# Memory keys and values by one plain float32 product in place of three rounded ones, in a two-layer streaming encoder step

## The chip, the cores and the metric

One NeuronCore of one Trainium2 chip runs the whole step as a single program. The metric is device time in microseconds (us). Its engines are named as the profile names them: PE (matmul; PEld are its weight loads), DVE (vector), ACT (scalar, with its own instruction queue), POOL (GpSimd, which also issues DMAs on a software queue) and SP (which issues only DMAs).

## The reference, cut to what matters

Two layers run over 512 prompt tokens and 32 sample tokens. Both layers attend into 256 memory rows, and the memory's keys and values for both layers come from one function, which does not depend on the tokens:

```python
def memory_kv(mem, mem_norm_g, w_mem_kv, mem_k_norm_g):
    Bsz, M, _ = mem.shape                      # M = 256, D = 1024
    m = rms_norm(mem[None], mem_norm_g[:, None, None, :])
    kv = jnp.einsum('lbmd,ldk->lbmk', m, w_mem_kv)   # 2 layers, 1024 -> 512
    k, v = jnp.split(kv, 2, axis=-1)
    k = rms_norm(k.reshape(DEPTH, Bsz, M, MEM_HEADS, MEM_HEAD_DIM), ...)
    return k, v.reshape(DEPTH, Bsz, M, MEM_HEADS, MEM_HEAD_DIM)
```

Everything is float32. The prompt's memory attention of layer 0 needs layer 0's keys and values, that of layer 1 needs layer 1's; both are outputs too.

## The kernel before, in words

Large products are made in three parts. A float32 operand is rounded to the one-instruction format float32r (the high part) and the rest is kept as a second float32r tile (the low part); the product is high by high, high by low and low by high, added in PSUM. For a weight tile, `weights` (L227) does this: SP loads the raw tile into a slot of the ring `wraw`, ACT writes the high part (L231) and the negated rounded copy (L232), and POOL issues a second DMA of the same weights that adds itself onto that copy (L233). The raw slot is put back at once, the high and low slots (rings `whi`, `wlo`) after the matmuls. Each ring has three slots.

The program's first stretch projects the tokens into layer 0 (`z0`, L324). Then comes the state-space stage (S5) of layer 0: six groups `m`, and for each a chain of small matmuls and transposes on PE (L681, L700, L729, L739, L752, L791, L792, L803), evacuations on ACT, table products and a scan on DVE (L669 to L696, L763 to L780), and a kernel matrix that POOL writes to DRAM (`kd<-kp`, L710) and reads back in eight small DMAs (L719) before the output products L791. After the last group the outputs are split, layer 0 attends into the memory (L430 to L520), and the product with `w_glu` starts the long dense part of the program: output projection, feed-forward, layer 1, feed-forward.

`mem_kv` (L334) is a generator whose pieces fill the S5 stage. Eight units (four pairs of 128 feature rows, two layers) each scale a pair of memory tiles by the norm's gain on ACT into a high part (L344), make the low part on DVE (L345), fetch a weight tile through `weights`, and issue 12 matmuls of 128 by 512 columns (L350): two row blocks, two feature tiles, three parts. That makes 96. Four PSUM banks collect the sums over all eight units. An epilogue then normalises the rows, writes both outputs and transposes the keys (L364 to L409).

The order on each engine is not the source order: a planner in the compiler orders the instructions by priority and by its own costs. The table `ORDER` moves blocks: the units of `mem_kv` have -60 (later than their place), its epilogue `mem_kv_end` 580 (earlier), the scans `s5_scan` 400. Engines then run their queues strictly in that order.

The memory units take their row tiles from the ring `rb`: four float32r tiles of 512 columns, made at L1004.

Of the kernel before, what the change touches and what calls it, by code (L numbers as in the profile page):

```python
# [9 lines left out]
F32 = mybir.dt.float32  # L10
F32R = mybir.dt.float32r
I32 = mybir.dt.int32
AF = mybir.ActivationFunctionType
ALU = mybir.AluOpType
# [4 lines left out]
KD = D // 128  # L19
# [8 lines left out]
NMEM = 256  # L28
# [109 lines left out]
def body(ctx, tc, A, O):  # L138
    nc = tc.nc
    V, S, P, T = nc.vector, nc.scalar, nc.gpsimd, nc.tensor  # L140
# [3 lines left out]
    FW = 576  # L144

    def slots(pool, n, dt, w, name):
        return Slots([pool.tile([128, w], dt, name=f"{name}{i}") for i in range(n)])
# [3 lines left out]
    R = None  # L151
    WR = slots(base, 3, F32, 1024, "wraw")
# [53 lines left out]
    def gcol(name, i):  # L206
        c = GP[name] + i
        return gp[:, c:c + 1]
# [18 lines left out]
    def weights(ap, *n, lo_eng=None):  # L227

        raw, hi, lo = WR.get(*n), WH.get(*n), WL.get(*n)
        nc.sync.dma_start(raw, ap)  # L230
        S.activation(hi, raw, AF.Copy)  # L231
        S.activation(lo, raw, AF.Copy, scale=-1.0)  # L232
        P.dma_start(lo, ap, accum_op=ALU.add)  # L233
        WR.put(raw)
        return hi, lo
# [8 lines left out]
    def wfree(w):  # L244
        WH.put(w[0])
        WL.put(w[1])
# [79 lines left out]
    def combos(a, b):  # L326
        return ((a[0], b[0]), (a[0], b[1]), (a[1], b[0]))
# [6 lines left out]
    def mem_kv(fm, rm, bm, b1, dst):  # L334
        ps = [[bm.get(512) for _ in range(2)] for _ in range(2)]
        acc = fm.get(2, NMEM)
        for u in range(4):
            mt = fm.get(2, NMEM)
            nc.sync.dma_start(mt, A["mem"][:, 2 * u:2 * u + 2, :])
            for l in range(2):  # L340
                hi, lo = rm.get(2, NMEM), rm.get(2, NMEM)
                for k2 in range(2):
                    g = gcol("mem", l * KD + 2 * u + k2)
                    S.activation(hi[:, k2], mt[:, k2], AF.Copy, scale=g)  # L344
                    V.scalar_tensor_tensor(lo[:, k2], mt[:, k2], g, hi[:, k2].bitcast(F32), ALU.mult, ALU.subtract)  # L345
                w = weights(A["w_mkv"][l, u], 1024, lo_eng=V if l else P)
                for t in range(2):
                    for k2 in range(2):
                        for i, (x, ww) in enumerate(combos((hi, lo), w)):
                            T.matmul(ps[l][t], x[:, k2, 128 * t:128 * t + 128], ww[:, 512 * k2:512 * k2 + 512],  # L350
                                     start=u == 0 and k2 == 0 and i == 0, stop=u == 3 and k2 == 1 and i == 2)
                wfree(w)
                rm.put(hi, lo)
                if l:
                    if u:
                        q = fm.get(2, NMEM)
                        S.activation(q, mt, AF.Square)
                        P.tensor_tensor(acc, acc, q, ALU.add)
                        fm.put(q)
                    else:  # L360
                        S.activation(acc, mt, AF.Square)
                    fm.put(mt)
                yield
        b = b1.get(512)  # L364
        for t in range(2):
            for u in range(2):
                T.matmul(b[:, t:t + 1], acc[:, u, 128 * t:128 * t + 128], ones, start=u == 0, stop=u == 1)
        x = sm(2, "mx", 1)
        V.tensor_scalar(x, b[:, :2], 1.0 / D, EPS, ALU.mult, ALU.add)
        b1.put(b)  # L370
        fm.put(acc)
        r = rsqrt(x, 128, 2, "mrs")
        yield
        for l in range(2):
            kt, v = dst[l]
            ss = sm(8, "mss")
            q = fm.get(2, 256)
            for t in range(2):
                S.activation(q[:, t], ps[l][t][:, :256], AF.Square, scale=r[:, t:t + 1])
                S.activation(v[:, t, :], ps[l][t][:, 256:], AF.Copy, scale=r[:, t:t + 1])  # L380
            V.tensor_reduce(ss, view(q, [[64, 8], [1, 64]]), AX.X, ALU.add)
            P.dma_start(O["mem_v"][l].rearrange("t p c -> p t c"), v)
            yield
            x = sm(8, "mkx")
            V.tensor_scalar(x, ss, 1.0 / 64, EPS, ALU.mult, ALU.add)
            y = rsqrt(x, 128, 8, "mkr")
            fm.put(q)
            V.tensor_tensor(y.rearrange("p (t h) -> p t h", t=2), y.rearrange("p (t h) -> p t h", t=2),
                            view(r, [[1, 2], [0, 4]]), ALU.mult)
            yield  # L390
            kk = fm.get(2, 256)
            for t in range(2):
                V.tensor_tensor(kk[:, t].rearrange("p (h d) -> p h d", d=64),
                                ps[l][t][:, :256].rearrange("p (h d) -> p h d", d=64),
                                view(y, [[1, 4], [0, 64]], 4 * t), ALU.mult)
            bm.put(*ps[l])
            kf = view(kk, [[64, 8], [1, 64]])
            V.tensor_tensor(kf, kf, view(grow(f"mk{l}"), [[0, 8], [1, 64]]), ALU.mult)
            P.dma_start(O["mem_k"][l].rearrange("t p c -> p t c"), kk)
            yield  # L400
            pt = b1.get(512)
            for hp in range(2):
                for t in range(2):
                    T.transpose(pt[:, 256 * hp + 128 * t:256 * hp + 128 * t + 128],
                                kk[:, t, 128 * hp:128 * hp + 128], ident)
            S.activation(kt.rearrange("p a b -> p (a b)"), pt, AF.Copy, scale=mqg[:, l:l + 1])
            b1.put(pt)
            fm.put(kk)
            yield  # L409
# [504 lines left out]
    lr = exr.enter_context(tc.tile_pool(name="l0r", bufs=1, reuse_waits="tile"))  # L914
    R = slots(lr, 16, F32R, NT, "ra")
# [73 lines left out]
    with pri("norm0"):  # L989
        rb = norm_bcast(r0, BS)  # L990
# [10 lines left out]
    exr.close()  # L1001
    exr = ExitStack()
    lr = exr.enter_context(tc.tile_pool(name="l0b", bufs=1, reuse_waits="tile"))
    R, fx = slots(lr, 4, F32R, 512, "rb"), slots(lr, 3, F32, FW, "fx")  # L1004
    FA, FB, FD = slots(lr, 2, F32, 1024, "wv"), slots(lr, 1, F32, 2 * FW, "tb"), slots(lr, 3, F32, 2 * FW, "wc")
    fxs = list(fx.free)
    F.merge(fx)
# [64 lines left out]
    lr = ctx.enter_context(tc.tile_pool(name="rc", bufs=1, reuse_waits="tile"))  # L1072
    R = slots(lr, 16, F32R, NT, "rc")
    bh = sm(NM, "bh", 1)
    V.tensor_scalar(bh, gp[:, GP["bglu"]:GP["bglu"] + NM], 0.5, None, ALU.mult)
    for y in ys:
        hi, lo = R.get(NT), R.get(NT)
# [7 lines left out]
    for m in range(NM):  # L1085
        if m in (1, 2, 4, 5):
            unit("mem_attend0", att)
        ps = BS.get(512), BS.get(512)
# [11 lines left out]
    for m in range(NM):  # L1100
        hi, lo = R.get(NT), R.get(NT)
# [38 lines left out]
    r1, rb = None, None  # L1140
    for m in range(8):
        ps = BG.get(512), BG.get(512)
        gemm(ps, xs, weights(A["w_in"][1, m], 1024))
        if rb is None:
            with pri("norm1"):
                r1, rb = norm_rows([acc], BM)
        if m < NM:
            hi, lo = R.get(NT), R.get(NT)
            sqt = zacc if m == 0 else F.get(NT)
            g = gcol("ql", m)  # L1150
# [21 lines left out]
    ps = BM.get(512)  # L1172
    stat_cols(zacc, ps)
    F.put(zacc)
    x = sm(5, "qx", 1)
# [625 lines left out]
```

## Time and profile before

| | us |
|---|---|
| median of three runs | 1451.76 (1451.24 to 1459.61) |
| the profiled execution, its own time | 1449.85 |
| span of that execution in the trace | 1448.1 |
| PE busy in the span | 1403.1 (97%) |
| DVE, ACT, POOL busy | 723.6, 755.9, 388.6 |

The profiled execution is 1.9 us under the median. A busy PE is not PE at its peak: matmuls overlap each other's fill and drain. PE is nearly full over the whole span but not over the stretch in which the memory projection lies, so its total share says little of this change. Stretches are given in us from the start of the span.

### The profile page before, as it was taken

How to read it: one execution, taken by the hardware profiler on the slowest of the kernel's cores; microseconds unless marked ns; L12 is line 12 of the kernel's file. 1: busy time of each engine (PE TensorE's matmuls, PEld its weight loads, DVE VectorE, ACT ScalarE, POOL GpSimd, SP SyncE). 2: the span in 40 equal slices, each digit the busy share in tenths (PEclk: the TensorE clock that was granted, in tenths of full speed). 3: DMA queues.
4: the chain of work that ended last, by engine and by line, in shares of the span. 5: the costliest groups of instructions: out<-in, count | busy, mean ns of one | idle time of the engine just before them, and what ended most of it. 6: DMA issues, size and time to landing. Idle time of an engine off the chain costs nothing.

```text
span 1448.1 us, 26899 instructions
## 1 busy us (share of the span) xinstructions
PE 1403.1 (97%) x10693; PEld 1310.7 (91%) x10693; DVE 723.6 (50%) x1810; ACT 755.9 (52%) x1247; POOL 388.6 (27%) x676
## 2 busy tenths in 40 slices
PE   7978799999999999999989999999999999999998
PEld 6966689999999999999988987557999999999998
DVE  7989742455514551455257655663355513551351
ACT  6656555565535553556555554654555534553452
POOL 2155432322111211124325421432322211221121
PEclk8999889999999999999999999999999999999999
DMA  9754637778788888869742432002778887888875
GB/s 268 163 142 121 155 75 175 169 164 175 176 179 171 176 176 178 173 141 207 158 120 62 124 102 60 11 20 57 165 171 177 177 175 172 176 177 174 176 157 139
DMA packets 67198, 214.80 MB, mean 148 GB/s; under 512 B 9280, under 2 KB 11552, under 8 KB 67072
## 3 DMA queue, kind: packets, MB, share of 16 engines
q0 software_dynamic: 30304, 100.81, 38.5%
q1 hardware_dynamic: 35616, 110.17, 26.5%
q10 hardware_dynamic: 1152, 2.10, 0.4%
q8 instruction: 84, 1.38, 0.4%
q14 instruction: 42, 0.34, 0.1%
HBM read 207.41 MB, written 5.61 MB: 147 GB/s over the span
## 4 chain that ended last, share of the span: by engine, by line
PE 82%; DVE 2%; DMA 2%; ACT 2%; issue 2%; POOL 1%; DVEq 0%; POOLq 0%; ACTq 0%
PE bank L324 64%; PE bank L1308 2%; PE bank L1556 2%; PE bank L1395 2%; PE bank L1592 1%; PE bank L1509 1%; PE bank L1483 1%; PE bank L1581 1%; DMA wlo<-i_w_f 1%; PE bank L1197 1%; PE bank L482 1%; PE bank L520 1%; PE bank L1423 1%; PE bank L510 0%; PE bank L1364 0%
## 5 line engine op out<-in xcount | busy, mean ns | idle before, releaser
L324 PE MATMUL bank<-rc,whi 128*128 128x272 f32 x3728 | 628.9, 290 | 0.2 <-DVE rc L305 0.2
L324 PEld LDWEIGHTS bank<-rc,whi 128*128 128x128 f32 x3728 | 530.3, 189 | 5.3 <-issue 4.3
L324 PE MATMUL bank<-rc,wlo 128*128 128x272 f32 x1864 | 389.4, 289 | 0.0
L231 ACT ACTIVATE whi<-wraw 128x1024 fp32r<-128x1024 f32 (+2 forms) x186 | 191.5, 1029 | 360.1 <-issue 311.3
L324 PEld LDWEIGHTS bank<-rc,wlo 128*128 128x128 f32 x1864 | 294.0, 189 | 0.4 <-issue 0.2
L324 PE MATMUL bank<-g,whi 128*128 128x272 f32 x1408 | 234.6, 288 | 0.8 <-ACT g L216 0.8
L324 PEld LDWEIGHTS bank<-g,whi 128*128 128x128 f32 x1408 | 198.8, 188 | 1.3 <-ACT g L216 1.2
L233 POOL DMA_DIRECT2D wlo<-i_w_f x136 | 117.5, 864 | 303.8 <-ACT wlo L232 300.5
L232 ACT ACTIVATE wlo<-wraw 128x1024 fp32r<-128x1024 f32 (+2 forms) x186 | 189.1, 1017 | 3.9 <-PE bank L350 3.3
L324 PE MATMUL bank<-g,wlo 128*128 128x272 f32 x704 | 145.8, 288 | 1.8 <-DMA wlo<-i_w_f 1.6
L851 DVE SCALAR_TENSOR_TENSOR fa<-fa,gp,fa 128x546 f32<-128x546 f32 x88 | 69.7, 792 | 139.8 <-ACT fa L850 139.8
L865 DVE TENSOR_TENSOR h<-bank,h 128x272 f32<-128x272 f32 x96 | 38.2, 436 | 172.3 <-PE bank L324 171.9
L324 PEld LDWEIGHTS bank<-g,wlo 128*128 128x128 f32 x704 | 110.4, 188 | 2.2 <-DMA wlo<-i_w_f 2.2
L850 ACT ACTIVATE fa<-fa,gp 128x546 f32<-128x546 f32 x88 | 73.2, 832 | 12.8 <-DVE fa L845 12.8
L843 DVE TENSOR_TENSOR fa<-bank,fa 128x272 f32<-128x272 f32 x88 | 38.9, 443 | 81.7 <-PE bank L324 77.5
L852 DVE SCALAR_TENSOR_TENSOR fa<-fa,gp,fa 128x546 f32<-128x546 f32 x88 | 69.5, 790 | 3.1
L891 ACT ACTIVATE fa<-fa 128x546 f32<-128x546 f32 x44 | 29.2, 663 | 71.7 <-DVE fa L852 71.7
L847 POOL COPY fa<-gp 128x2 f32<-128x2 f32 x88 | 19.0, 216 | 168.3 <-DVE g L217 107.7
L848 POOL COPY fa<-fa 128x4 f32<-128x4 f32 x88 | 18.2, 207 | 165.2 <-DVE fa L845 165.2
L324 PE MATMUL bank<-ra,whi 128*128 128x272 f32 x256 | 47.5, 307 | 3.1 <-ACT whi L241 3.1
L216 ACT ACTIVATE g<-fa 128x544 fp32r<-128x544 f32 x44 | 29.0, 659 | 37.6 <-DVE fa L893 37.6
L892 DVE TENSOR_TENSOR fa<-fa,fa 128x512 f32<-128x512 f32 x44 | 30.5, 693 | 33.6 <-ACT fa L891 33.6
(629 smaller groups left out, 2020.3 us busy)
## 6 DMA issues: line engine op xcount, KB each, us to landing
wraw<-i_w_f SPq DMA_DIRECT2D x120, 512.0 KB, 4.9
wlo<-i_w_f POOLq DMA_DIRECT2D x120, 512.0 KB, 7.4
wraw<-i_w_out SPq DMA_DIRECT2D x16, 512.0 KB, 4.3
wlo<-i_w_out POOLq DMA_DIRECT2D x16, 512.0 KB, 7.1
wraw<-i_w_in SPq DMA_DIRECT2D x14, 512.0 KB, 5.0
wlo<-i_w_in POOLq DMA_DIRECT2D x14, 512.0 KB, 7.7
wraw<-i_w_f SPq DMA_DIRECT2D x16, 384.0 KB, 3.4
wlo<-i_w_f POOLq DMA_DIRECT2D x16, 384.0 KB, 6.3
```

What stands on the lines that cost most here:

```text
L216: S.activation(hi, src, AF.Copy)
L231: S.activation(hi, raw, AF.Copy)
L232: S.activation(lo, raw, AF.Copy, scale=-1.0)
L233: P.dma_start(lo, ap, accum_op=ALU.add)
L324: T.matmul(ps[q][:, :c], ww, xx[:, c0:c0 + c], start=k == 0 and i == 0, stop=k == n - 1 and i == 2)
L843: V.tensor_tensor(u[:, 2:274], ps[0][:, :272], rb[:, :272], ALU.mult)
L850: S.activation(y, u[:, 2:548], AF.Identity, scale=gcol("cw", 3 * ci + 2), bias=gcol("cb", ci))
L851: V.scalar_tensor_tensor(y, u[:, 1:547], gcol("cw", 3 * ci + 1), y, ALU.mult, ALU.add)
L852: V.scalar_tensor_tensor(y, u[:, 0:546], gcol("cw", 3 * ci), y, ALU.mult, ALU.add)
L865: V.tensor_tensor(h[m][:, c0:c0 + cc], ps[qd][:, :cc], h[m][:, c0:c0 + cc], ALU.add)
L891: S.activation(yg, yg, AF.Silu)
L892: V.tensor_tensor(u[:, 2:514], ya[:, :NP], yg[:, :NP], ALU.mult)
```

## The change

The row tiles are scaled into one plain float32 tile, the raw weight tile is loaded and used as it is, and each product is one float32 matmul call in place of three float32r ones. The low part of the rows (DVE), the two conversions of the weights (ACT) and the adding DMA (POOL) of this projection go. The raw weight slot is put back after the matmuls of its unit and no longer right after the conversions; the rings of high and low weights aren't used here any more. The ring `rb` becomes two float32 tiles. All other products keep their three parts.

```diff
             for l in range(2):
-                hi, lo = rm.get(2, NMEM), rm.get(2, NMEM)
+                x, w = rm.get(2, NMEM), WR.get(1024)
+                nc.sync.dma_start(w, A["w_mkv"][l, u])
                 for k2 in range(2):
-                    g = gcol("mem", l * KD + 2 * u + k2)
-                    S.activation(hi[:, k2], mt[:, k2], AF.Copy, scale=g)
-                    V.scalar_tensor_tensor(lo[:, k2], mt[:, k2], g, hi[:, k2].bitcast(F32), ALU.mult, ALU.subtract)
-                w = weights(A["w_mkv"][l, u], 1024, lo_eng=V if l else P)
+                    S.activation(x[:, k2], mt[:, k2], AF.Copy, scale=gcol("mem", l * KD + 2 * u + k2))
                 for t in range(2):
                     for k2 in range(2):
-                        for i, (x, ww) in enumerate(combos((hi, lo), w)):
-                            T.matmul(ps[l][t], x[:, k2, 128 * t:128 * t + 128], ww[:, 512 * k2:512 * k2 + 512],
-                                     start=u == 0 and k2 == 0 and i == 0, stop=u == 3 and k2 == 1 and i == 2)
-                wfree(w)
-                rm.put(hi, lo)
+                        T.matmul(ps[l][t], x[:, k2, 128 * t:128 * t + 128], w[:, 512 * k2:512 * k2 + 512],
+                                 start=u == 0 and k2 == 0, stop=u == 3 and k2 == 1)
+                WR.put(w)
+                rm.put(x)
...
-    R, fx = slots(lr, 4, F32R, 512, "rb"), slots(lr, 3, F32, FW, "fx")
+    R, fx = slots(lr, 2, F32, 512, "rb"), slots(lr, 3, F32, FW, "fx")
```

## Rows read from the trace of the kernel before

**Rows 1.** The page: span, busy time of the engines.

```profile
span 1448.1 us, 26899 instructions
PE 1403.1 (97%) x10693; PEld 1310.7 (91%) x10693; DVE 723.6 (50%) x1810; ACT 755.9 (52%) x1247; POOL 388.6 (27%) x676
```

**Rows 2.** Windows: length, busy of PE, PEld, DVE, ACT, POOL, clock, DMA.

```profile
72.00:96.70 24.70, 17.98 (x148) 15.15 (x145) 24.54 (x43) 12.41 (x29) 12.94 (x24) 0.86 0.60 142
102.10:150.20 48.10, 40.63 (x403) 32.92 (x398) 47.86 (x78) 31.68 (x75) 29.37 (x49) 1.00 0.58 136
150.20:168.00 17.80, 13.97 (x101) 11.87 (x101) 12.67 (x42) 9.38 (x25) 9.13 (x17) 0.90 0.69 174
66.00:168.00 102.00, 83.30 (x769) 69.03 (x767) 90.53 (x170) 63.99 (x146) 55.61 (x97) 0.95 0.60 143
184.00:1448.00 1264.00, 1249.83 (x9469) 1178.05 (x9468) 568.12 (x1413) 644.57 (x1026) 316.36 (x547) 1.00 0.66 145
```

**Rows 3.** Groups by shape, 60 to 215 us: removed ACT and POOL work.

```profile
L232 ACT ACTIVATE wlo<-wraw 128x1024 fp32r<-128x1024 f32 x7 | 7.4, 1061 | 2.0 <-PE bank L350 2.0
L231 ACT ACTIVATE whi<-wraw 128x1024 fp32r<-128x1024 f32 x7 | 7.4, 1057 | 3.3 <-issue 2.5 <-PE bank L350 0.6 <-ACT fx L361 0.2
L233 POOL DMA_DIRECT2D wlo<-i_w_mkv x7 | 6.5, 936 | 13.8 <-ACT wlo L232 13.8
```

**Rows 4.** Timeline of DVE: start, duration, instruction, idle before and releaser.

```profile
102.11 0.45 DVE L763 TENSOR_TENSOR fa<-bank,tab 128x276 f32<-128x276 f32 x1 [5.38 <-ACT wlo L232]
...
112.14 0.48 DVE L345 SCALAR_TENSOR_TENSOR rb<-fa,gp,rb 128x256 fp32r<-128x256 f32 x1
112.54 0.69 DVE L672 TENSOR_TENSOR wv<-wv,tb 128x512 f32<-128x512 f32 x1
...
147.48 1.50 DVE L345 SCALAR_TENSOR_TENSOR rb<-fa,gp,rb 128x256 fp32r<-128x256 f32 x1
148.90 1.34 DVE L696 TENSOR_TENSOR wc<-wc,tb 128x1152 f32<-128x1152 f32 x1
```

**Rows 5.** Window of line L345 alone: DVE busy and its count.

```profile
60.00:215.00 155.00, 8.65 (x16) 0.91 0.53 127
```

**Rows 6.** Timeline of PE: three-part products, memory projection; first w_glu matmul.

```profile
98.07 0.87 PE L350 MATMUL bank<-whi,rb 128*128 128x512 f32 x3
98.78 0.40 PE L350 MATMUL bank<-wlo,rb 128*128 128x512 f32 x1
...
184.01 0.82 PE L324 MATMUL bank<-rc,whi 128*128 128x272 f32 x2
```

**Rows 7.** Groups by shape, 870 to 1000 us: plain float32 products.

```profile
L1556 PE MATMUL bank<-fe,fa 96*128 96x512 f32 x4 | 2.0, 592 | 0.0
L1556 PE MATMUL bank<-fe,fa 96*128 96x128 f32 x4 | 0.8, 274 | 0.0
```

**Rows 8.** Line L449: min/median/max ns, first and last start.

```profile
L449 PE MATMUL bank<-fa,fa x8: 379/379/462, 171.3 to 889.3; 128*128 128x256 f32 x8
```

**Rows 9.** Waits from 66 to 168 us: total, times, longest.

```profile
POOL fa L719 <- DMA kd<-kp: 18.6, 4, 6.7
```

**Rows 10.** Timeline of POOL around the fifth kernel matrix.

```profile
137.41 0.61 POOL L710 DMA_DIRECT2D kd<-kp  x1 [0.30 <-POOL kp L707]
...
140.43 3.56 POOL L719 DMA_DIRECT2D fa<-kd  x6 [0.35 <-issue]
```

**Rows 11.** The chain that ended last: start, us, piece.

```profile
140.18 0.94 ACT whi L231
...
144.17 1.82 PE bank L350 x7
...
152.03 4.42 DMA kd<-kp
...
157.00 4.63 DMA fa<-kd
```

**Rows 12.** Timeline of SP's queue: start, us, DMA issues, count.

```profile
144.49 26.49 SPq L230 DMA_DIRECT2D wraw<-i_w_glu  x4
```

## The prediction

> **What bounds the kernel now.** I read the page first. PE is busy for 97% of the span, so one expects that anything which lengthens PE's work lengthens the kernel, and that work on other engines is free [rows 1]. That holds for the dense part, where PE is busy for 1249.83 of 1264 us. The windows show that it does not hold where the changed lines are [rows 2]. All the memory matmuls lie between 72 and 168 us. From 66 to 168 us PE is busy for 83.3 of 102 us and DVE for 90.5; from 72 to 96.7 us DVE is busy for 24.54 of 24.70 us, and from 102.1 to 150.2 us for 47.86 of 48.10. In these two stretches DVE is the bound: the table products and scans of the six groups queue there back to back, and the low parts of the memory rows stand between them. Between the two DVE waits 5.38 us for the first product of the third group [rows 4]. After 150 us DVE has room again, and the last kernel matrix's way through DRAM sets the end [rows 11].
>
> So the change takes work from the stage's bound and gives work to the engine that is next to it. The question is how much of what DVE gives back PE takes.
>
> **PE.** Before, the projection is 96 matmuls of 512 columns. Undisturbed they start 0.237 us apart: three from 98.07 to 98.78 us [rows 6]. That is 96 x 0.237 = 22.8 us. After, there are 32 products in plain float32. The trace has no such product of 128 by 128 by 512, but it has smaller ones. Line L449 issues two products in each of two layers, four in all, and shows eight instructions: a plain product is two instructions [rows 8]. In L1556 the instruction takes 592 ns at 512 columns and 274 at 128, so a column costs (592 - 274) / 384 = 0.828 ns and 512 columns 0.424 us [rows 7]. The part that doesn't grow overlaps with the neighbour, as it does in L350, where matmuls of 0.40 us start every 0.237 us. I take 0.433 us, the slope and 9 ns of spacing; the lower end is 0.424, the upper 0.592 if nothing overlaps. 64 x 0.433 = 27.7 us, which is 4.9 us more than before (4.3 to 15.1). In rows 66 to 168 us PE rises to 88.2 us and DVE falls to 81.9: PE becomes the busiest engine of the stage.
>
> The Trainium skill has a rule by which this term has the other sign: "Perfetto Trace Analysis", section Engine Utilization, gives the matmul rate with a footnote that float32 in its low-and-high form runs at half the rate, as one reads it two cycles for a column of a product. By it the 32 products would be 32 x 0.433 = 13.9 us and PE 8.9 us lighter. The eight instructions for four products speak against reading it for a whole product, and for reading it for each of two [rows 8]; its time is a rival below.
>
> **DVE.** The sixteen instructions of L345 go, 8.65 us of busy time [rows 5]. What they hold of the queue is the step to the next start: 0.40 us (112.14 to 112.54), and once 1.42 us, at 147.48, where it ran slowly [rows 4]. Five of them lie in the first full stretch: 5 x 0.40 = 2.0 us. Eight lie in the second: 7 x 0.40 + 1.42 = 4.2 us. Three lie after 150 us, where DVE is busy for 12.67 of 17.80 us; they are worth nothing [rows 2].
>
> In the first stretch PE is busy for 17.98 of 24.70 us, and a sixth of its added work, 0.8 us, fits: I take the 2.0 us whole. In the second PE stands at 40.63 us. About half of the memory matmuls are there, so it gets some 2.5 us more: 43.1 us. If the stretch shrank by all of 4.2 us to 43.9, PE would have to be 98% busy, as full as in the dense part, in a stretch where it waits for ACT and DVE between small matmuls. If PE reached only 91.5%, midway between today's 84% and the dense part's 99%, the stretch would be 47.1 us and the gain 1.0. I take the middle of 1.0 and 4.2, which is 2.6 us.
>
> **The 5.38 us stall.** The row names a weight conversion on ACT as what ended it [rows 4]. ACT runs in order, and a conversion of 1.06 us ahead of an evacuation holds up the transposes, the scan's products and so DVE. Without conversions ACT is free there, but PE's memory matmuls stand in the same chain and get longer by about a quarter. Bounds: 0 to 5.4 us; I take 0, since the one conversion (1.06) and the added matmul time are of one size.
>
> **ACT and POOL.** Seven conversions of each kind from 60 us on, 14 x 1.06 = 14.8 us of ACT, and seven adding DMAs, 6.5 us of POOL, go [rows 3]. Neither is the bound: 63.99 and 55.61 us of 102 [rows 2]. The bytes go too. POOL's queue waits 18.6 us in four times for the kernel matrix to land in DRAM, at worst 6.7 us [rows 9]. With no adding DMA near, the fifth goes out at 137.41 and its reads begin at 140.43, at most 3.0 us later [rows 10]. So the round trips of the early groups should shorten by 2 to 4 us each. What hides that today is DVE's queue: group outputs wait for the scan. I cost it at 0, and it is worth up to what the stall rival takes.
>
> **The end of the stage.** On the chain from 137.50 to 162.11 us stand 16 memory matmuls in five pieces, the longest 1.82 us [rows 11]. They would cost 16 x 0.237 = 3.8 us before, and 16 / 3 x 0.866 = 4.6 after: 0.8 us more. The conversion at 140.18, 0.94 us, leaves the same chain. Sum -0.1 us. The chain then runs through the last matrix, 4.42 us to DRAM and 4.63 us back, which the change doesn't touch.
>
> **The moved release.** A raw weight slot is now held until its unit's matmuls. SP issues in order, so the loads of `w_glu` queue behind the third last, second last and last unit. Before, four such loads went out between 144.49 and 170.98 us [rows 12], while the first matmul that needs any starts at 184.01 [rows 6]. A load that waits until the last unit, at 166 us, is no later than the last of these. Cost 0; if the projection slipped past 175 us, its delay would come through. Two tiles in place of four in the ring `rb` are two units, as before: 0.
>
> **Sum.** -2.0 - 2.6 - 0.1 = -4.7 us. The profiled execution gives 1449.85 - 4.7 = 1445.15; the median of the runs lies 1.9 us higher, so 1451.76 - 4.7 = 1447.1 us. After 184 us nothing changes.
>
> **Rivals.**
> PE takes over and the kernel is slower. The place is the S5 stage, the price the added 4.9 us, and it decides when PE's 18.7 idle us (102 - 83.3) are forced by round trips in which no memory matmul is ready, so that every added matmul delays a transpose. For it: PE would be the busiest engine, and five pieces of the memory matmuls are on the chain already. Against: the planner places them late, in gaps. Time 1456.7.
> Everything is given back. DVE's 7.4 us of queue (15 x 0.40 + 1.42) and the stall of 5.4 go, with shorter round trips: -12.8 us, 1439.0. PE would then be busy for 88.2 of 89.2 us; that is the ceiling, and few stages of small matmuls come near it.
> No change: the last matrix's path and the small steps of ACT set the pace, and DVE's full queue only follows. For it: a DVE that works all the time may be working on the planner's early tables. Time 1451.8, within 1 us.
> Half-rate products: if a plain product were one instruction of 0.433 us, PE would not take anything of DVE's 6.2 us; time 1445.6. The count of L449 speaks against it. Behind it stands the Trainium skill, "Perfetto Trace Analysis", Engine Utilization, read for a whole product.
> That the change doesn't do what it says can be at one point: the planner, with other costs, reorders the six groups, by one round trip of the matrix (4.4 to 6.7 us) either way [rows 9, 11].
>
> **How the numbers follow.** Forecast (1444 to 1450) 0.45; PE takes over 0.20; no change 0.15; everything given back 0.13; half-rate products 0.02; a reorder or matmuls that don't overlap (+15.1 us) 0.05. One per cent, about what a measurement of this kernel can tell from no change, is 14.5 us: only the upper end of the matmul cost, at 1466.9, and a full gain with a round trip on top pass it. Faster 0.05, within 0.91, slower 0.04. The range takes in the forecast, no change and PE taking over, and most of the way to the full gain: 1440 to 1457 us, which leaves out some 0.15. The most likely case alone has 1444 to 1450.
>
> **What would show it.** 64 memory matmuls, starting 0.43 us apart; no L345, no low weights of this projection; DVE's full stretches shorter by 6 us or less, PE's share in the stage near 90%; the first `w_glu` matmul at about 179 us and the same 1264 us behind it. It would be wrong if that matmul moved by more than 8 us, if products started further apart than 0.45 us, or if the part behind 184 us changed its length.

## The result, and the profile after

The kernel after takes 1437.86 us (median of 5 runs, 1437.09 to 1438.81), the kernel before, run beside it, 1453.32 (5 runs, 1451.24 to 1459.61). The ratio is 0.9884, with a 95% interval of 0.9857 to 0.9911: 15.5 us less, where 4.7 were forecast. The profiled executions have spans of 1435.0 and 1448.1 us, 13.1 apart; what follows divides these 13.1. Lines below the projection have numbers lower by 3 in the kernel after: the scan's first product, L763, is L760 there.

The page after, its busy times, which answer to [rows 1]:

```profile
span 1435.0 us, 26790 instructions
PE 1405.1 (98%) x10661; PEld 1302.8 (91%) x10661; DVE 714.8 (50%) x1794; ACT 740.2 (52%) x1231; POOL 381.2 (27%) x668
```

PE works 2.0 us more in all and the kernel is 13.1 us shorter. The windows after are cut at the first scan product (L760) of the first group at 70.3, of the third at 94.1 and of the sixth at 143.8, at the first product on the memory's keys (L427) at 163.0, and at the first of `w_glu` (length; busy of PE, PEld, DVE, ACT, POOL; clock; DMA share; GB/s):

```profile
70.30:94.10 23.80, 22.95 (x207) 15.46 (x203) 23.64 (x41) 14.10 (x33) 15.84 (x30) 1.00 0.42 122
94.10:143.80 49.70, 43.81 (x372) 30.91 (x373) 45.27 (x74) 26.64 (x69) 26.43 (x46) 0.93 0.37 104
143.80:163.00 19.20, 16.05 (x123) 11.39 (x117) 15.77 (x61) 13.42 (x35) 10.38 (x20) 0.96 0.71 190
...
171.50:1435.00 1263.50, 1250.54 (x9469) 1178.45 (x9468) 565.87 (x1416) 644.39 (x1026) 315.44 (x547) 0.99 0.65 145
```

The kernel before, cut at the same instructions (the middle one stands in [rows 2]):

```profile
71.30:102.10 30.80, 23.52 (x211) 19.50 (x209) 25.22 (x44) 17.82 (x37) 17.11 (x32) 0.89 0.54 129
...
150.20:175.40 25.20, 16.92 (x117) 13.86 (x117) 19.37 (x72) 14.39 (x35) 11.43 (x20) 0.87 0.64 168
```

So: 30.8 to 23.8 (7.0 less), 48.1 to 49.7 (1.6 more), 25.2 to 19.2 (6.0 less). The start gives 1.1, the part behind `w_glu` 0.6. The gain lies at the two ends, and in both the granted clock rose, from 0.89 to 1.00 and from 0.87 to 0.96. In the long middle stretch, the second full one of the prediction, DVE's busy time fell by 2.6 us, yet the stretch became longer and the clock fell, from 1.00 to 0.93. DVE works there almost without a break up to 137 us and then stands 4.20 us for PE, which itself has stood 3.24 us for the fifth kernel matrix (DVE, then PE, in the kernel after):

```profile
141.25 0.73 DVE L217 TENSOR_TENSOR rc<-fa,rc 128x544 fp32r<-128x544 f32 x1 [4.20 <-PE bank L678]
...
136.46 0.67 PE L788 MATMUL bank<-fa,fa 128*69 128x128 f32 x2 [3.24 <-DMA fa<-kd]
```

So what DVE gave back in this stretch was lost again behind the fifth matrix's way through DRAM, though none of the adding DMAs is left here.

The forecast rows, on PE and DVE after, answer to [rows 4, 6]. DVE:

```profile
94.13 0.43 DVE L760 TENSOR_TENSOR fa<-bank,tab 128x276 f32<-128x276 f32 x1
```

PE:

```profile
101.51 2.74 PE L347 MATMUL bank<-wraw,rb 128*128 128x512 f32 x6
...
171.52 0.82 PE L324 MATMUL bank<-rc,whi 128*128 128x272 f32 x2
```

The third group's scan waits for nothing; the 5.38 us are gone. Six instructions of plain products take 2.74 us: five steps of some 0.43 and an end. The first `w_glu` matmul comes 12.5 us earlier.

What changed at the first end is seen from the kernel matrices. The DMA view (KB each, median us from issue to landing) of the kernel before, 66 to 160 us:

```profile
wlo<-i_w_mkv POOLq DMA_DIRECT2D x6, 512.0 KB, 7.8
...
kd<-kp POOLq DMA_DIRECT2D x6, 240.0 KB, 5.5
```

and of the kernel after:

```profile
kd<-kp POOLq DMA_DIRECT2D x6, 240.0 KB, 2.5
```

POOL's waits after, which answer to [rows 9]:

```profile
POOL fa L716 <- DMA kd<-kp: 8.9, 4, 3.0
```

One such round trip in full, for the first group. POOL's timeline of the kernel before (start, duration, instruction, idle before it and what ended that):

```profile
72.13 0.86 POOL L233 DMA_DIRECT2D wlo<-i_w_mkv  x1 [6.64 <-ACT wlo L232]
73.64 0.62 POOL L710 DMA_DIRECT2D kd<-kp  x1 [0.30 <-POOL kp L707]
79.59 1.86 POOL L719 DMA_DIRECT2D fa<-kd  x3 [4.57 <-DMA kd<-kp]
```

ACT's and PE's, a little later:

```profile
84.42 0.38 ACT L731 ACTIVATE fa<-bank 69x256 f32<-69x256 f32 x1 [2.83 <-POOL kp L707]
```

```profile
84.86 0.72 PE L739 MATMUL bank<-cn,big 69*128 69x69 f32 x4 [4.01 <-ACT fa L731]
...
85.83 0.63 PE L791 MATMUL bank<-fa,fa 128*69 128x128 f32 x2
86.26 0.63 PE L792 MATMUL bank<-wc,fx 128*69 128x128 f32 x2
```

and the windows of PE's idle time and of the output products behind it, and of those behind the sixth group's matrix:

```profile
80.70:84.80 4.10, 0.14 (x2) 0.00 (x0) 4.04 (x11) 1.03 (x3) 4.10 (x10) 0.87 0.44 107
85.80:89.40 3.60, 3.60 (x20) 3.60 (x19) 3.56 (x8) 0.67 (x1) 1.19 (x4) 0.50 0.62 107
...
161.80:165.50 3.70, 3.70 (x18) 3.46 (x19) 1.32 (x4) 0.00 (x0) 2.64 (x4) 0.56 0.27 67
```

Read as a chain: the adding DMA goes out at 72.13, the matrix is written 1.5 us behind it and read only at 79.59. POOL, in order, has stood 4.57 us for it. Seven of its eight read issues then stand ahead of the second group's `kp` (L707), for which ACT waits 2.83 us and PE, through ACT, 4.01. After this idle time PE runs at 1.2 GHz: pairs of output products start 0.43 us apart, at a granted clock of 0.50. The same in the kernel after, POOL and PE:

```profile
72.12 0.62 POOL L707 DMA_DIRECT2D kd<-kp  x1 [0.30 <-POOL kp L704]
74.77 3.61 POOL L716 DMA_DIRECT2D fa<-kd  x6 [0.89 <-DMA kd<-kp]
```

```profile
82.32 0.38 PE L788 MATMUL bank<-fa,fa 128*69 128x128 f32 x2
82.54 0.38 PE L789 MATMUL bank<-wc,fx 128*69 128x128 f32 x2
```

2.65 us in place of 5.95, and pairs 0.22 us apart, which is 2.4 GHz. At the other end PE stood 3.70 us for the sixth matrix before and then ran at 0.56; after, it stands 1.48 and runs at 1.00 from 153.8 to 157.9 us. The first output product of the sixth group, before and after:

```profile
161.67 0.44 PE L791 MATMUL bank<-fa,fa 128*69 128x128 f32 x2 [3.70 <-DMA fa<-kd]
```

```profile
153.72 0.44 PE L788 MATMUL bank<-fa,fa 128*69 128x128 f32 x2 [1.48 <-DMA fa<-kd]
```

### The profile page after: what moved, and what is told of

It reads as the page before. It is cut to its first block, busy times and chain, and to the rows that moved or that the text cites. A ratio compares the mean times of both kernels' runs of the same rounds, so it can differ in the third digit from the quotient of the medians.

```text
span 1435.0 us, 26790 instructions
## 1 busy us (share of the span) xinstructions
PE 1405.1 (98%) x10661; PEld 1302.8 (91%) x10661; DVE 714.8 (50%) x1794; ACT 740.2 (52%) x1231; POOL 381.2 (27%) x668
## 3 DMA queue, kind: packets, MB, share of 16 engines
q1 hardware_dynamic: 35616, 110.17, 26.5%
## 4 chain that ended last, share of the span: by engine, by line
PE 86%; DVE 4%; DMA 4%; ACT 3%; issue 2%; POOL 1%; SPq 0%; DVEq 0%; POOLq 0%; ACTq 0%
PE bank L324 67%; PE bank L1305 3%; PE bank L1553 2%; PE bank L1392 2%; PE bank L1589 1%; DMA wlo<-i_w_in 1%; PE bank L1506 1%; PE bank L1480 1%; PE bank L1578 1%; PE bank L1194 1%; PE bank L479 1%; DMA wlo<-i_w_f 1%; PE bank L517 1%; PE bank L1420 1%; DMA kd<-kp 1%
## 5 line engine op out<-in xcount | busy, mean ns | idle before, releaser
L231 ACT ACTIVATE whi<-wraw 128x1024 fp32r<-128x1024 f32 (+2 forms) x178 | 182.8, 1027 | 351.1 <-issue 304.7
L232 ACT ACTIVATE wlo<-wraw 128x1024 fp32r<-128x1024 f32 (+2 forms) x178 | 180.6, 1014 | 0.6 <-PE bank L1506 0.5
L844 POOL COPY fa<-gp 128x2 f32<-128x2 f32 x88 | 18.6, 212 | 170.4 <-DVE g L217 105.1
```

## The experiments

Theories at the start: DVE's queue is the bound and its relief is the gain (the prediction's reason); against it, the weight staging delays the S5 chain (conversions on ACT, adding DMAs among the matrix round trips), or PE is the bound. Each kernel was run 4 to 12 times, in five sets, and the kernel before beside each set: medians 1453.1, 1454.2, 1453.6, 1453.6 and 1453.4 us. A difference from the kernel before goes by the median of the same set. Intervals on differences are 95%, from the means of the runs.

**Give one engine's work back to the kernel after.** DVE's low parts, read by nobody:

```diff
+                    V.scalar_tensor_tensor(lo[:, k2], mt[:, k2], gcol(...), x[:, k2], ALU.mult, ALU.subtract)
```

> The changed kernel with the sixteen DVE instructions of the row low parts put back; they write tiles that nothing reads. The changed kernel took 1437.9 us, the one before 1453.3. Theory A (the gain is mostly ACT and POOL work taken out of the in-order queues, which ended the 5.4 us stall and shortened the end of the stage; DVE's relief is worth the 2 us of the first full stretch): 1439 to 1442. Theory B (DVE was the bound and its 7.4 us of queue are about half of the gain): 1444 to 1447. Theory C (any edit makes the planner lay out the stage anew, and the new layout is what is faster): no fixed amount, and the stage's order would differ from the changed kernel's in more than the added instructions.

1437.13 us (1435.77 to 1441.7): nothing, where the kernel after itself has 1437.86. ACT's two conversions, read by nobody:

```diff
+                S.activation(wh, w, AF.Copy)
+                S.activation(wl, w, AF.Copy, scale=-1.0)
```

> The changed kernel with both ACT conversions of each weight tile put back (sixteen instructions of 128 by 1024, some 17 us of ACT); they write tiles that nothing reads, and they wait for no matmul. Theory A: the stall before the third group's first product returns in part and the end gets longer: 1444 to 1450. Theory B: ACT is not the bound (58 of 110 us busy): 1437 to 1440. Theory C: no fixed amount.

1440.97 us (1433.9 to 1446.15), 3.1 us more within a wide spread. A second load of each weight block by POOL, plain and read by nobody:

```diff
+                P.dma_start(wl, A["w_mkv"][l, u])
```

> The changed kernel with a second DMA of each weight tile on POOL's queue put back, a plain copy into tiles that nothing reads (8 x 512 KB). Theory A: the kernel matrix's way through DRAM gets its 2 to 4 us per group back, seen on the chain in the later groups: 1440 to 1444. Theory B: hidden, 1437 to 1439. Theory C: no fixed amount.

1432.62 us (1431.81 to 1433.23): 5.2 less, with more work. But nothing holds these loads back, and the last of them went out at 37.1 us, before the first kernel matrix at 78.1; they don't test the staging at its old places. Together: no engine's busy time, given back alone, brings the gain back; whether ACT's 3.1 us are anything the spread leaves open.

**Take one part from the kernel before.** The low rows away; the second product uses the high part:

```diff
-                    V.scalar_tensor_tensor(lo[:, k2], mt[:, k2], g, hi[:, k2].bitcast(F32), ALU.mult, ALU.subtract)
...
-                        for i, (x, ww) in enumerate(combos((hi, lo), w)):
+                        for i, (x, ww) in enumerate(combos((hi, hi), w)):
```

> The kernel before without the low part of the memory rows: the second product of three uses the high part again, so that PE, ACT and POOL do what they did and only DVE loses its sixteen instructions. Left out: the low part of the memory rows. Theory A: 2 to 4 us off, 1449 to 1451. Theory B: 7 us or more off, 1444 to 1446. Theory C: no fixed amount.

1450.22 us, ratio 0.998 (0.9958 to 1.0002): 2.9 less, which is not clear of nothing. The adding DMA away, all else there:

```diff
-    def weights(ap, *n, lo_eng=None):
+    def weights(ap, *n, lo_eng=None, add=True):
...
-        P.dma_start(lo, ap, accum_op=ALU.add)
+        if add:
+            P.dma_start(lo, ap, accum_op=ALU.add)
...
-                w = weights(A["w_mkv"][l, u], 1024, lo_eng=V if l else P)
+                w = weights(A["w_mkv"][l, u], 1024, add=False)
```

> The kernel before without POOL's adding DMA of this projection's weights; both ACT conversions, the low rows on DVE, all 96 matmuls and the waits between ACT and PE stay. Left out: the weights' low part (the negated rounded copy is multiplied instead). Theory A, narrowed after the first four runs to POOL's queue: each adding DMA stands ahead of a kernel matrix on the same software queue, so that the matrix lands 3 to 5 us late, and POOL itself stands waiting for ACT's copy, which waits for PE. The gain then comes back without any other part of the change: 1440 to 1446, and the matrix's write to first read falls from 6 to 8 us to about 3. Theory C (any other layout by the planner is as good): no fixed amount. Theory D (the plain matmuls keep PE filled and so its granted clock up; the queues don't matter): 1450 to 1454.

1446.8 us, ratio 0.9943 (0.9921 to 0.9965): 7.4 less, though it keeps ACT's, DVE's and PE's work. Its DMA view, 66 to 160 us:

```profile
kd<-kp POOLq DMA_DIRECT2D x6, 240.0 KB, 2.4
```

The matrices land as fast as in the kernel after, and from 66 to 100 us the granted clock is 1.00, where before has 0.90. One converting POOL DMA in place of raw load, conversions and adding DMA:

```diff
-                w = weights(A["w_mkv"][l, u], 1024, lo_eng=V if l else P)
+                wr = WH.get(1024)
+                P.dma_start(wr, A["w_mkv"][l, u])
+                w = wr, wr
...
-                wfree(w)
+                WH.put(wr)
```

> The kernel before with one converting DMA on POOL's queue in place of the raw load, both ACT conversions and the adding DMA; the result serves as high and as low part, so all 96 matmuls and the low rows stay. POOL still issues eight DMAs of 512 KB and still waits for PE's slots, but no longer for ACT. Left out: the weights' low part. Theory A: ACT is freed, and the queue is still shared, so part of the gain: 1444 to 1450. Theory D: 1450 to 1454.

1444.79 us: 9.4 less than before, 2.0 less than without the adding DMA alone. This DMA too is POOL's, and lands in 3.9 us against the adding one's 7.8; the matrices' median landing is 2.5, with one such DMA close ahead of only one of the six.

**Is it the queue?** The matrix written from SP's queue in the kernel before, its reads left on POOL's:

```diff
-        P.dma_start(q["kd"][m], kp)
+        nc.sync.dma_start(q["kd"][m], kp)
```

> The kernel before with the six kernel matrices written to DRAM by SP's queue and no longer by POOL's; nothing else. The result is the reference's. Theory A: the write no longer stands behind the adding DMA, the reads still do and POOL still waits for ACT: 1444 to 1450. Theory D: 1450 to 1454; SP's queue might even hold weight loads back.

1458.2 us, 4.0 more. Its DMA view, 66 to 160 us (the profiled execution took 1467.1 us, the slowest of its twelve):

```profile
wlo<-i_w_mkv POOLq DMA_DIRECT2D x6, 512.0 KB, 8.1
...
kd<-kp SPq DMA_DIRECT2D x5, 240.0 KB, 6.9
```

From another queue the write lands no sooner. Later the reads were moved too, on both kernels:

```diff
-                P.dma_start(kk[gh][:, i], ...)
+                nc.sync.dma_start(kk[gh][:, i], ...)
```

> The kernel before with the kernel matrices' write and their eight reads a group issued on SP's queue in place of POOL's; all else stays. Theory of the queue (the round trip waits behind adding DMAs): write to first read falls to some 3 us in all groups, 1443 to 1449. Theory of POOL's own waiting or of DMA traffic: the time stays within 3 us of before. Rival: SP, which issues in order and stands for buffers of weight loads, delays write or reads, 1454 to 1462.

> The same edit on the kernel after, which has no adding DMA in front of five of the six groups' round trips. Theory of the queue: little to gain, the sixth group's 1.9 us at most, 1435 to 1439. Rival: SP's order delays the round trips, 1440 to 1450.

1455.54 us on the kernel before, ratio 1.0004 (0.9985 to 1.0024), and 1437.77 on the kernel after: nothing on either. The timelines of the kernel before with this edit show why, POOL and SP's queue:

```profile
102.61 0.88 POOL L233 DMA_DIRECT2D wlo<-i_w_mkv  x1 [3.83 <-ACT wlo L232]
```

```profile
104.67 0.33 SPq L710 DMA_DIRECT2D kd<-kp  x1
110.12 5.17 SPq L719 DMA_DIRECT2D big<-kd  x8
```

5.45 us from write to read behind an adding DMA of POOL's queue, and 2.07 in the fifth group, which has none near. The theory that POOL's queue is the place falls: an adding DMA just ahead delays the write from either queue. POOL's own standing falls too as the only way into the chain, for here POOL no longer stands for the landing and nothing is gained. The wait comes in at ACT as well, whose copy of a group into `kp`, a single tile, stands until the write of the group before has landed (waits of this run, 66 to 168 us):

```profile
ACT kp L706 <- DMA kd<-kp: 1.1, 1, 1.1
```

Nor does it take an adding DMA. In the run with converting DMAs the one that goes out 1.72 us ahead of the fifth matrix does it too (POOL's timeline):

```profile
129.09 0.58 POOL L347 DMA_DIRECT2D whi<-i_w_mkv  x1 [0.89 <-PE bank L352]
...
130.81 0.59 POOL L712 DMA_DIRECT2D kd<-kp  x1 [0.30 <-POOL kp L709]
...
135.76 4.15 POOL L721 DMA_DIRECT2D fa<-kd  x7 [2.36 <-DMA kd<-kp]
```

This write landed after 4.7 us, the four before it after 2.3 to 3.1. In the run with second loads SP's plain load of a weight block, 1.35 us ahead of the second matrix, left it 4.5 us. The adding DMA is the worst of the three: it takes 7.8 us, and in the kernel before one goes out 0.6 to 2.9 us ahead of four of the six matrices.

The Trainium skill has a mechanism that would fit, "DMA: Bandwidth & Descriptors", section "Queues, rings and completion order": the queues are rings on the same sixteen DMA engines, served in turn, and a completion is reported only after all earlier writes of that DMA engine, those of other queues too. The 6.9 and 5.45 us agree; no run here shows the ordering by itself.

**Is PE the bound?** 32 products of float32r in the kernel after, weights by a converting POOL DMA:

```diff
-                x, w = rm.get(2, NMEM), WR.get(1024)
-                nc.sync.dma_start(w, A["w_mkv"][l, u])
+                x, w = rm.get(2, NMEM), WH.get(1024)
+                P.dma_start(w, A["w_mkv"][l, u])
...
-    R, fx = slots(lr, 2, F32, 512, "rb"), slots(lr, 3, F32, FW, "fx")
+    R, fx = slots(lr, 2, F32R, 512, "rb"), slots(lr, 3, F32, FW, "fx")
```

> The changed kernel with one float32r matmul in place of each plain float32 product (32 instead of 64 instructions, each at half the cost: about 20 us of PE less); the rows are rounded by ACT as they are scaled, the weights by one converting DMA on POOL. Left out: all low parts. If PE bounds the stage of the changed kernel (it is busy for 43.8 of 49.7 us between the third and the last group's scan): 1425 to 1433. Theory A with PE off the path: 1435 to 1441, since eight DMAs are on POOL's queue again. Theory D: slower than the changed kernel, 1440 to 1446, as PE's gaps let the granted clock fall.

1441.43 us (1439.39 to 1442.77): 3.6 more than after, though PE is busy for 88.79 of the 114 us from 66 to 180, against 103.98. So PE's busy time is not the bound. This kernel also issues eight converting DMAs on POOL's queue, one of them 1.53 us ahead of the second matrix, which landed after 4.9 us; the pair that differs in the products comes below, and so does what the granted clock, 0.81 against 0.91, goes with.

**The staging with its waits.** What the first runs had left out: in the kernel after, products stay plain, but read staged weights, so that the staging again waits for PE and PE for it. With the adding DMA; the second run leaves it out as above:

```diff
-                x, w = rm.get(2, NMEM), WR.get(1024)
-                nc.sync.dma_start(w, A["w_mkv"][l, u])
+                x, w = rm.get(2, NMEM), weights(A["w_mkv"][l, u], 1024)
...
-                        T.matmul(ps[l][t], x[...], w[:, 512 * k2:512 * k2 + 512],
+                        T.matmul(ps[l][t], x[...], w[k2].bitcast(F32)[:, 512 * k2:512 * k2 + 512],
```

> The kernel after, its 32 plain products kept, but each weight block staged as before the change: raw load, two ACT conversions into the ring slots, the POOL adding DMA. The products read the high part for the first half of a block and the low part for the second, so that they wait for what they waited for before; the output is not the product of the weights. The rows' low parts stay away. Theory of the waits (ring slot, conversions, adding DMA ahead of the kernel matrices' traffic on the same queue): some 8 to 13 us of the 15.5 come back, 1446 to 1451, matrix write to read again 5 us or more in several groups. Theory of the matmul's form (plain products keep PE at its clock, two products fewer): no more than 3 us come back, 1438 to 1441.

> As the run with staged weights on the kernel after, but without the adding DMA: the products read the high part, and for the second half of a block the negated high part, so the output is not the product of the weights. What is left of the chain are the conversions and their waits for a ring slot. If the adding DMA's place on the queue makes half of the gain, as its removal from the kernel before said (7.4 us): 5 to 8 us under the run with it, 1439 to 1444. If the conversions' wait for PE is the larger part: within 3 us of the run with it.

1446.11 us (1441.58 to 1447.46) with it, 1433.75 (1432.44 to 1437.08) without: 12.4 apart by the medians, 10.7 +- 3.0 by the means. The DMA view, 66 to 160 us, with it:

```profile
kd<-kp POOLq DMA_DIRECT2D x6, 240.0 KB, 6.4
```

and without it:

```profile
kd<-kp POOLq DMA_DIRECT2D x6, 240.0 KB, 2.6
```

The conversions, with all their waits for ring slots, cost nothing here: 4.1 us less than the kernel after.

The stall before the third group's first scan product follows the adding DMA. The kernel before without it, and the kernel after with staging and with it:

```profile
98.55 0.45 DVE L764 TENSOR_TENSOR fa<-bank,tab 128x276 f32<-128x276 f32 x1 [0.47 <-ACT wlo L232]
```

```profile
104.26 0.44 DVE L759 TENSOR_TENSOR fa<-bank,tab 128x276 f32<-128x276 f32 x1 [8.48 <-PE bank L748]
```

It is 4.7 to 8.5 us long in all six kernels of this document that hold these adding DMAs, the two with traffic moved to SP's queue among them, and at most 1.5 us in the others, but for 3.8 in the one with converting DMAs and 32 rounded products. Stalls of 3.5 to 5.9 us before a later group's scan stay in four kernels without the adding DMA. The stretch from the first group's scan to the third's is 26.8 us in place of 30.8 in the first of these two; in the second it is 32.3 us, and 23.1 when the adding DMA goes. The end of the stage does not follow it: from the sixth group's scan to the first `w_glu` matmul the kernel before takes 33.8 us, and 35.5 without the adding DMA; the kernel after takes 27.7, and 27.2 with staging and adding DMA.

**Does the planner's order do it?** One number, on either kernel:

```diff
-"mem_kv": -60,
+"mem_kv": -200,
```

> The kernel after with nothing changed but one number of the planner, the due time offset of the memory units, -60 to -200, which sets the memory products at other places among the groups. It tells how much the order alone moves. Theory of the waits: under 5 us, 1434 to 1442. Theory of the order (the change gained because the planner laid the stage out anew): up to 15 us to either side.

> The kernel before with the same one number, -60 to -200. Theory of the waits: the adding DMAs stand ahead of the kernel matrices' traffic wherever the memory units lie, so the time stays within 5 us of before, above 1448. Theory of the order: another place alone could bring it to 1440 or under.

1435.96 us (1.9 less) and 1460.71 (7.1 more, ratio 1.0036, 1.0018 to 1.0055). The order did not make the gain, but the same work laid out anew moves by 2 to 7 us. A single pair of kernels that differs by less says little, and neither this 1435.96 nor the 1432.62 of the run with second loads (ratio 0.9863, 0.9837 to 0.989) can be called a better version than the kernel after.

**The rest.** With the staging, but no adding DMA: 96 rounded products without low rows, 32 rounded, and 32 plain with the low rows' DVE instructions (the first two, cut to the lines that matter; the third joins the staged plain products with the DVE line of the first run):

```diff
-                w = weights(A["w_mkv"][l, u], 1024, lo_eng=V if l else P)
+                w = weights(A["w_mkv"][l, u], 1024, add=False)
...
-                        for i, (x, ww) in enumerate(combos((hi, lo), w)):
+                        for i, (x, ww) in enumerate(combos((hi, hi), w)):       # 96
+                        for i, (x, ww) in enumerate(((hi, w[k2]),)):            # 32
```

> The kernel before without the adding DMA and without the rows' low parts on DVE; the two conversions and the 96 rounded products stay, on high parts of the rows alone, so the output is not the product of rows and weights. Against the run before without adding DMA (1446.8) it lacks only the 16 DVE instructions; against the kernel after with staging and no adding DMA (1433.8) it differs only in the products. If the low rows on DVE were the rest of the gain: 1434 to 1439. If the product's form and number were: 1442 to 1448.

> The same with 32 rounded products in place of 96: high part of the rows by the high part of the weights for the first half of a block, by the negated high part for the second, so the output is not the product. It holds the least PE work of all. If the number of products (PE's busy time, instructions in PE's queue) is the rest of the gain: 1432 to 1437, no slower than the 32 plain ones. If plain products help by themselves, by keeping PE filled: 1440 to 1446, as the run with one rounded product on the kernel after (1441.4).

> The kernel after with staging and no adding DMA (plain products, output not the product), and the 16 DVE instructions for the rows' low parts put back, their result read by nobody. If DVE's work is the rest of the gain: 1438 to 1446. If it is not, as the runs that took it from before and gave it back to after said: 1433 to 1437.

1440.0, 1442.62 and 1444.3 us. With the earlier runs, every part now has several pairs of kernels that differ in it and in little else (those made from the kernel after with plain products convert the weights before they scale the rows, the others the other way round). Medians; intervals of the means in brackets:

| part taken away | pairs | us |
|---|---|---|
| adding DMA | from before; without low rows; with plain products | -7.4 (+-2.2), -10.2 (+-4.1), -12.4 (+-3.0) |
| low rows on DVE | from before; without adding DMA, 96 products; the same, plain | -2.9 (+-3.4), -6.8 (+-3.1), -10.5 (+-2.6) |
| 96 rounded to 32 plain products | with low rows, no adding DMA; no low rows, with it; neither | -2.5 (+-2.0), -4.1 (+-3.7), -6.2 (+-3.5) |
| conversions | from the run with 1433.75 to after; from the one with 1444.3 to the first run, low rows alone given back | +4.1, -7.2 |

One way from before to after, without the adding DMA, then without low rows, then plain, then without conversions: -7.4 - 6.8 - 6.2 + 4.1 = -16.3, against 15.5 measured. Some of these values, the -2.5, -2.9 and 4.1 above all, lie within what a new layout alone moves. The conversions have no steady sign, and low rows that cost 10.5 us beside conversions cost nothing without them (the first run): layout, or ACT and DVE together, which these runs don't part.

What goes with the 8.9 us that 32 rounded products take longer than 32 plain ones (8.6 +- 3.2 by the means; the profiled executions are 11.3 apart) is in the rows. Windows from 66 to 180 us and groups of the small S5 matmuls there (busy, mean ns), with rounded products:

```profile
66.00:180.00 114.00, 87.25 (x760) 75.55 (x759) 92.67 (x192) 67.86 (x157) 58.83 (x94) 0.81 0.42 112
```

```profile
L791 PE MATMUL bank<-fa,fa 128*69 128x128 f32 x48 | 13.4, 375 | 2.8 <-ACT fa L683 1.9 <-ACT kp L706 0.5 <-DMA fa<-kd 0.4
...
L681 PE MATMUL bank<-cn,wv 128*128 128x128 f32 x48 | 9.2, 334 | 0.0
```

and with plain ones:

```profile
66.00:180.00 114.00, 102.71 (x849) 78.38 (x848) 97.58 (x210) 73.17 (x168) 56.11 (x99) 0.94 0.41 111
```

```profile
L788 PE MATMUL bank<-fa,fa 128*69 128x128 f32 x48 | 11.0, 317 | 3.5 <-DMA fa<-kd 3.5
...
L678 PE MATMUL bank<-cn,wv 128*128 128x128 f32 x48 | 7.3, 278 | 1.6 <-DVE wv L669 1.6
```

The same instructions, as many of them, take longer: all shapes of L681, L791, L792 and L803 sum to 63.7 us, against 53.6. PE, busy for 87.25 us in place of 102.71, runs more of them at 1.2 GHz, and these 10.1 us are of the size of the loss; that they are the loss no run shows. By the Trainium skill, "TensorE: Matmul & The Clock Gate", section "What's actually happening", the gate follows how busy PE has lately been; the trace agrees, 0.81 against 0.94. The clock does not explain 96 rounded against 32 plain: there the same sum is 53.8, and the 6.2 us stay open.

## Why the prediction was wrong

**ACT and POOL, "I cost it at 0": the step that failed.** It had the right rows: round trips of up to 6.7 us where one with no adding DMA near took 3.0 [rows 9, 10], "shorten by 2 to 4 us each". The median landing went from 5.5 to 2.5, and POOL's standing for it from 23.4 us to 9.5 (the 18.6 of [rows 9] leave out one wait of 4.7 into another tile). But the prediction hid all that behind DVE's queue, and there it failed: a matrix that lands late holds back the next group's `kp`, in the kernel before through POOL, which works in order, with it ACT and PE, and only through them DVE. Taking the adding DMA away is worth 7.4 us in the kernel before, and 10 to 12 in two kernels around it.

**The stall, "I take 0".** The 5.4 us went whole. The prediction looked for the cause in the conversion of 1.06 us that the row names [rows 4] and set longer matmuls against it. What the scan product reads is made by L752 on PE, which in the kernel before began only at 101.30:

```profile
101.30 0.71 PE L752 MATMUL bank<-fa,fx 128*64 128x69 f32 x16 [0.28 <-ACT fa L683]
```

The chain from the adding DMA at 72.13 to PE's idle 4.01 and 3.6 us at half clock lies before that, and without the adding DMA the stall goes even where the conversions stay (0.47 us).

**The end of the stage, -0.1.** 6.0 us came here, which no rival had. The prediction followed the last matrix's 4.42 and 4.63 us [rows 11] and left out what PE does behind them: 3.70 us idle and output products at a clock of 0.56. From write to first read the trip is hardly shorter (4.57 us in place of 4.97, in both behind an adding DMA of `w_glu`), from first read to first output product it is 3.44 in place of 4.67. Some 1.6 of the 6.0 us lie ahead of that product and 4.5 behind it, where PE's clock and the epilogue of the memory are. The adding DMA of this projection is not their cause, as the runs above show; what is stays open.

**DVE as the bound.** Windows of the kernel after with the low rows given back, the first and the second full stretch:

```profile
70.70:97.20 26.50, 25.58 (x212) 16.14 (x208) 26.34 (x46) 14.18 (x33) 15.37 (x30) 1.00 0.45 129
97.20:143.20 46.00, 37.99 (x361) 27.68 (x362) 45.77 (x76) 26.27 (x69) 25.48 (x45) 1.00 0.41 110
```

The first stretch, -2.0, is borne out in this pair: 26.5 us with the low rows, 23.8 without. The second, -2.6, became 1.6 longer. DVE does fill it in the kernel before (47.86 of 48.10 us) and here (45.77 of 46.00); wrong was that its relief must shorten it, for in the kernel after PE's wait for the fifth matrix and its lower clock took over. In all, the same instructions given back cost nothing. Taken from the kernel before, they give 2.9 us and, without adding DMAs, 6.8; the forecast's 4.6 lies between.

**PE, +4.9.** The count and the spacing held: 64 instructions, 2.74 us for six. What was wrong is the sign of what they do to the time. Plain products are no slower than the 96 rounded ones in any of three pairs, but 2.5 to 6.2 us faster, about what a new layout can move, and 8.9 faster than 32 rounded ones. So "PE takes over" falls, and with it the bound of 91.5% in the second stretch; the half-rate rival falls by the count.

**The moved release and the rest after 184 us** were right: 1264.1 and 1263.5 us behind the first `w_glu` matmul. The prediction's own sign of being wrong came there too: this matmul moved by 12.5 us, where it allowed 8.

**Everything given back**, 1439.0, came within 1.2 us of the result, partly by luck, with half of its reason: the stall was in it, the 4.2 us of DVE's second stretch were not to be had, and the end was missing. The share of 0.13 was too small because DVE's full queue was taken for a cover; the range's lower end, 1440, missed by 2.1 us.

## What to carry to other kernels

Before a shorter wait is costed at nothing, follow the engine that waits: an engine that works in order holds back everything behind the wait, a tile that is still being read holds back whoever fills it next, and a full queue on another engine is no cover if that engine is fed through the first. A small write that is read back at once should not go out close behind a large DMA, an accumulating one above all, from any queue. And idle time of PE is paid for twice where PE then restarts at 1.2 GHz, so the window's clock column should be read beside its busy columns.

## What the runs showed of the hardware that was not expected

- The 240 KB write of a kernel matrix lands, by the medians of the kernels, 5.3 to 6.5 us after issue on POOL's queue where 512 KB accumulating DMAs go out among the matrices, and after 6.9 on SP's; in kernels without them after 2.4 to 2.8. The accumulating DMA takes 7.8 us, a converting one of the same size 3.9. A converting DMA 1.72 us ahead left the write 4.7 us, a plain load 1.35 us ahead 4.5.
- With 32 rounded in place of 32 plain products PE's busy time for them fell from 33.4 us (16.7 for each half of the weights) to 14.8 (7.3 and 7.5), and the kernel became 8.9 us slower, at a granted clock of 0.81 in place of 0.94.
